# Modulation weights of a two-block transformer: as halves in activation tiles, one column group ahead, instead of through the ring of raw weight tiles

## Chip, cores and metric

One Trainium2 chip, one core. The metric is the device time of the slowest core (here the only one), in microseconds (us); the median of several runs is given. The granted clock of TensorE is told as a share of full speed, 2.4 GHz; its other level is 1.2 GHz.

## What is computed

`reference` chains two blocks over 256 tokens of width 1024, in float32. The first block (two layers: FFN, RWKV and block-sparse attention mixer, cross attention, FFN) is the same before and after. The second block is the one with modulation:

```python
mod_lat = (silu(c) @ w_mod[i] + b_mod[i])[:, None, :]
mod_ctx = (silu(c_ctx) @ w_mod[i] + b_mod[i])[None, None, :]
sh1, sc1, gt1, sh2, sc2, gt2 = split(mod_lat, 6, axis=-1)
csh1, csc1, cgt1, csh2, csc2, cgt2 = split(mod_ctx, 6, axis=-1)
...
x_lat = x_lat + gt1 * mix
x_lat = x_lat + gt2 * sq_relu_mlp(modulate(rms_norm_2(x_lat, g_norm2[i]), sh2, sc2), w_mlp1[i], w_mlp2[i])
```

It has two layers (i = 0, 1), 256 latent tokens and 256 context tokens. `w_mod` is 2 x 1024 x 6144 float32, 50 MB of weights that are multiplied by two vectors only. `mix` is a grouped-query attention, a low-rank attention and a pooling, concatenated and projected by `w_out`. The context is not updated in the last layer.

## The kernel before

The kernel is bound by matmuls in float32 accuracy: each product is three passes, `mm3` (L537, L538, L539), on operands split into a high and a low part. Weights stream from HBM in tiles of 128 x 1024 (512 KB). `raw` (L484) takes a tile from a ring of four (NRAW) and issues its DMA on SP's queue (L486); `wsplit` makes the high part on ScalarE (L513) and the low part on VectorE (L514), three pairs at a time; then the matmuls use them. SP issues in order: a load that waits for its tile holds up the loads behind it.

The modulation weights are read by `mod_vectors(l, half)` (L1388). A half of a layer has 12 column groups, so there are 48 groups in all, numbered here 0 to 47 over (0,0), (0,1), (1,0), (1,1). Before, a group is two raw tiles, from the same ring of four, and they are not split: eight float32 matmuls (L1399) read them directly, with the two small vectors as the 32-column operand, four of them side by side in four column quadrants of PE (`tile_position`):

```python
ws = [self.raw(self.t["mod"][(l * 24 + n) * 2 + kc]) for kc in range(2)]
for kc in range(2):
    for q in range(4):
        nc.tensor.matmul(ps[32 * q:32 * q + 32, :S], self.cs[:, 4 * kc + q, ...],
                         ws[kc][:, q * S:q * S + S], ..., tile_position=(0, 32 * q))
```

A matmul in float32 leaves two records in the trace, so a whole group is one row with x16. After the twelfth group of a half the sums are copied, transposed and added to the bias.

Where the groups stand: the generator is a background stream. `wload` (L489 to L499) advances it by a count of units at each weight tile (`due`), so one group comes with every few weight tiles. The halves (0,0), (0,1) and what fits of (1,0) run so in the first block's FFNs and mixers (`early`, L1362); the rest of (1,0) in the first MLP of the second block (L1997). The last half, (1,1), is a side stream (`modulation`, L2032 to L2036) of the weave of the second block's second layer (L2038), which interleaves projections, attention, keys, queries and pooling. Its result is needed after the last out projection, `mix_out(1, lat)` (L2040), by the norm ahead of the last MLP (`lat["h"].finish()`, L2041).

The order on each engine is not the program's: a scheduler places instructions by priority and by when it expects operands and pool slots to be free. A tile that is to be written waits until the slot's earlier reader is done. The activation pool (`b2`, L415) has 55 slots (NB2) of 128 x 512 (256 KB); hidden activations, keys, queries and probabilities live there.

Of the kernel before, what the change touches and what calls it, by code (L numbers as in the profile page):

```python
# [19 lines left out]
S = 256  # L20
# [1350 lines left out]
class Second(First):  # L1371
# [16 lines left out]
    def mod_vectors(self, l, half, bank=None):  # L1388

        nc = self.nc  # L1390
        bank = bank or self.at_ps
        for n in range(12 * half, 12 * half + 12):
            m = n % MG
            if m == 0:
                ps = bank()
            ws = [self.raw(self.t["mod"][(l * 24 + n) * 2 + kc]) for kc in range(2)]
            for kc in range(2):
                for q in range(4):
                    nc.tensor.matmul(ps[32 * q:32 * q + 32, :S], self.cs[:, 4 * kc + q, 32 - 2 * m:64 - 2 * m],  # L1399
                                     ws[kc][:, q * S:q * S + S], start=m == 0 and kc == 0,  # L1400
                                     stop=m == MG - 1 and kc == 1, tile_position=(0, 32 * q))
            if m < MG - 1:
                yield 2 * self.mpace
                continue
            sb = self.t1()
            nc.scalar.activation(sb, ps[:, :S], AF.Copy)
            yield U
            pt = bank()
            for b in range(2):
                nc.tensor.matmul(pt[:, 32 * b:32 * b + 32], sb[:, b * P:(b + 1) * P], self.cst("sel32"),  # L1410
                                 start=True, stop=True)
            for b in range(2):
                blocks = slice(2 * (n - m) + b, 2 * n + b + 1, 2)
                nc.vector.tensor_tensor(self.mods[l][:, blocks],
                                        pt[:, 32 * b:32 * b + 2 * MG].rearrange("p (m i) -> p m i", i=2),
                                        self.vec(f"b_mod{l}")[:, blocks].unsqueeze(2).to_broadcast([P, MG, 2]),
                                        op=ALU.add)
            yield 2 * self.mpace - U
            if n - m <= 12 * half + 7 <= n:
                o, i = 24 * half + 8, half + 1  # L1420
                self.gm[l][i] = g = self.cp.tile([P, KD, 2], F32, name=f"gm{i}_{l}")
                nc.vector.scalar_tensor_tensor(g, self.mods[l][:, o:o + 8], 1.0,
                                               self.vec(f"g_norm{i}{l}").unsqueeze(2).to_broadcast([P, KD, 2]),
                                               op0=ALU.add, op1=ALU.mult)
        self.modulated.add((l, half))
# [650 lines left out]
```

## Time and profile before

| | us |
|---|---|
| median of 3 runs | 2471.49 (2471.09 to 2473.09) |
| the profiled execution | 2474.53 |
| its span in the profile | 2472.7 |
| mean granted clock in it | 0.983 |

The profile shows one execution, and its rows are in us from the start of the span. In it a busy time is that of the instructions of one engine; an idle time stands in brackets behind the instruction that came after it, with what released it ("<-DMA raw<-in_mod_dram": the load of a modulation tile). Rows of matmuls overlap, so the start of the next row tells more than a row's duration. A window row gives a stretch and its length, then the busy time and the instructions (x) of PE, PEld, DVE, ACT and POOL in it, then PE's granted clock, the busy share of the DMA engines and their GB/s. PEld is the load of PE's stationary operand.

### The profile page before, as it was taken

Reading aid. Unit: us, or ns where it says so; the run is one execution under the profiler, and the core shown is the slowest. Engines: PE = TensorE matmul, PEld = TensorE weight load, DVE = VectorE, ACT = ScalarE, POOL = GpSimd, SP = SyncE. Lnnn points to the kernel's source line nnn. Section 1 sums busy time; section 2 is a strip of 40 time slices with the busy share of each in tenths; the row PEclk is TensorE's granted clock in tenths of the full one; section 3 lists DMA queues with packets and bytes.
Section 4 is the critical chain, followed back from the end, with each engine's and each line's share of the span. In section 5 each row is a group of like instructions: output and inputs, shape, how many; then the busy total and the mean of one; then the engine's idle time right before and its main releaser. Section 6 shows DMA issues by size and latency. Waiting matters only on the chain. (4 is left out here: it accounts for less than half of the span.)

```text
span 2472.7 us, 52358 instructions
## 1 busy us (share of the span) xinstructions
PE 2373.1 (96%) x21745; PEld 2254.9 (91%) x21745; DVE 1627.8 (66%) x2883; ACT 1187.2 (48%) x2025; POOL 260.4 (11%) x396
## 2 busy tenths in 40 slices
PE   8999999999999999999999999879999999788999
PEld 7998889999999998889999989869999999668999
DVE  6756767666556657757686777877753447776665
ACT  5544346544444445355554565556542235454443
POOL 2210101011001101001021121120100003021000
PEclk9999999999999999999999999989999999889999
DMA  6766333467776775334455534412672226442554
GB/s 217 225 224 201 118 107 101 142 189 229 223 237 220 224 231 170 100 99 121 137 182 168 176 120 137 142 60 86 195 231 95 93 87 214 154 131 69 179 179 146
DMA packets 115310, 393.17 MB, mean 159 GB/s; under 512 B 12864, under 2 KB 16704, under 8 KB 115072
## 3 DMA queue, kind: packets, MB, share of 16 engines
q1 hardware_dynamic: 113920, 388.15, 49.5%
q8 instruction: 171, 2.80, 0.4%
q10 hardware_dynamic: 1152, 1.67, 0.2%
q14 instruction: 67, 0.55, 0.1%
HBM read 388.71 MB, written 3.16 MB: 158 GB/s over the span
## 5 line engine op out<-in xcount | busy, mean ns | idle before, releaser
L537 PE MATMUL mm<-b,wh 128*128 128x256 f32 x4792 | 1375.6, 288 | 21.4 <-ACT wh L518 7.7
L538 PE MATMUL mm<-b,wh 128*128 128x256 f32 x4792 | 1364.1, 285 | 1.4 <-DVE b L531 1.4
L539 PE MATMUL mm<-b,wl 128*128 128x256 f32 x4792 | 1361.5, 284 | 3.0 <-DVE wl L514 2.8
L513 ACT ACTIVATE wh<-raw 128x1024 fp32r<-128x1024 f32 (+2 forms) x637 | 658.1, 1034 | 889.7 <-PE mm L538 470.3
L514 DVE TENSOR_TENSOR wl<-raw,wh 128x1024 fp32r<-128x1024 f32 (+2 forms) x637 | 766.6, 1205 | 448.0 <-ACT wh L513 442.5
L537 PEld LDWEIGHTS mm<-b,wh 128*128 128x128 f32 x4792 | 921.9, 193 | 48.4 <-issue 18.9
L539 PEld LDWEIGHTS mm<-b,wl 128*128 128x128 f32 x4792 | 922.6, 193 | 6.2 <-DVE wl L514 4.5
L538 PEld LDWEIGHTS mm<-b,wh 128*128 128x128 f32 x4792 | 923.1, 193 | 4.1 <-DVE b L531 2.6
L639 POOL TENSOR_TENSOR t<-t,t 128x256 f32<-128x256 f32 x85 | 85.4, 1007 | 896.3 <-ACT t L636 895.6
L518 ACT ACTIVATE b<-t 128x256 fp32r<-128x256 f32 (+1 forms) x192 | 86.4, 462 | 111.4 <-POOL t L789 66.2
L519 DVE TENSOR_TENSOR b<-t,b 128x256 fp32r<-128x256 f32 (+1 forms) x192 | 93.8, 498 | 57.4 <-ACT b L518 57.3
L789 POOL TENSOR_TENSOR t<-t,t 128x256 f32<-128x256 f32 x88 | 71.3, 810 | 468.5 <-DVE t L787 422.8
L784 DVE TENSOR_TENSOR t<-mm,rb 128x512 f32<-128x512 f32 x88 | 60.6, 689 | 35.3 <-PE mm L539 33.9
L537 PE MATMUL mm<-wh,b 128*128 128x256 f32 (+2 forms) x272 | 81.5, 302 | 1.6 <-ACT wh L513 1.1
L538 PE MATMUL mm<-wl,b 128*128 128x256 f32 (+2 forms) x272 | 80.0, 295 | 0.8 <-DVE wl L514 0.8
L539 PE MATMUL mm<-wh,b 128*128 128x256 f32 (+2 forms) x272 | 79.1, 294 | 0.5 <-DVE b L376 0.5
L537 PE MATMUL at<-b,b 64*128 64x256 f32 (+3 forms) x216 | 66.7, 315 | 9.9 <-ACT b L654 4.9
L538 PE MATMUL at<-b,b 128*128 128x256 f32 (+3 forms) x240 | 69.2, 293 | 0.0
L1399 PE MATMUL at<-raw,cs 128*32 128x256 f32 x768 | 60.5, 396 | 8.5 <-DMA raw<-in_mod_dram 8.5
L654 ACT ACTIVATE b<-at,mx 128x512 f32<-128x512 f32 (+1 forms) x88 | 51.2, 587 | 32.2 <-DVE mx L1303 17.9
L1839 DVE SCALAR_TENSOR_TENSOR x<-mm,mods,x 128x256 f32<-128x256 f32 x80 | 38.5, 482 | 41.6 <-PE mm L539 41.4
L539 PE MATMUL at<-b,b 64*128 64x256 f32 (+3 forms) x216 | 62.2, 294 | 1.1 <-DVE b L519 1.1
(296 smaller groups left out, 2518.0 us busy)
## 6 DMA issues: line engine op xcount, KB each, us to landing
raw<-in_ffn_in_dram SPq DMA_DIRECT2D x175, 512.0 KB, 4.0
raw<-in_mlp_dram SPq DMA_DIRECT2D x160, 512.0 KB, 3.4
raw<-in_mod_dram SPq DMA_DIRECT2D x96, 512.0 KB, 4.1
raw<-in_ffn_out_dram SPq DMA_DIRECT2D x64, 512.0 KB, 4.3
raw<-in_mix_in_dram SPq DMA_DIRECT2D x52, 512.0 KB, 3.9
raw<-in_xkv_dram SPq DMA_DIRECT2D x32, 512.0 KB, 3.6
raw<-in_ffn_out_dram SPq DMA_DIRECT2D x32, 384.0 KB, 3.4
raw<-in_out_dram SPq DMA_DIRECT2D x24, 512.0 KB, 4.0
```

The lines of the kernel that those rows point to most:

```text
L513: nc.scalar.activation(wh[:, :width], raw[:, :width], AF.Copy)
L514: nc.vector.tensor_tensor(wl[:, :width], raw[:, :width], wh[:, :width].bitcast(F32), op=ALU.subtract)
L518: self.nc.scalar.activation(h, src, AF.Copy)
L519: self.nc.vector.tensor_tensor(l, src, h.bitcast(F32), op=ALU.subtract)
L537: mm(out, a[0], b[0], start=first, stop=False)
L538: mm(out, a[0], b[1], start=False, stop=False)
L539: mm(out, a[1], b[0], start=False, stop=last)
L639: eng.tensor_tensor(sqs[0], sqs[0], sq, op=ALU.add)
L654: nc.scalar.activation(p, s, AF.Exp, scale=scale, bias=neg, accum_out=sm)
L784: nc.vector.tensor_tensor(gu, self.pair(ps), self.over2(norm.rb), op=ALU.mult)
L789: nc.gpsimd.tensor_tensor(hv, th, gu[:, 1], op=ALU.mult)
L1399: nc.tensor.matmul(ps[32 * q:32 * q + 32, :S], self.cs[:, 4 * kc + q, 32 - 2 * m:64 - 2 * m], ws[kc][:, q * S:q * S + S], start=m == 0 and ...
```

## The change

A group is now four tiles of the activation pool (`b2`, 128 x 2 x 256, 256 KB each, half a raw tile), each with a DMA of its own (L1397 of the changed kernel). `load(n + 1)` is called ahead of the matmuls of group n; the first group of each half is loaded in the step that uses it. The eight matmuls of a group (L1408 now) are the same, with the same values. The ring of raw tiles holds only split weights. Lines behind this place are 9 higher.

```diff
@@ -1389,15 +1389,24 @@
 
         nc = self.nc
         bank = bank or self.at_ps
+
+        def load(n):
+            ws = [self.b2() for _ in range(4)]
+            for i, w in enumerate(ws):
+                src = self.t["mod"][(l * 24 + n) * 2 + i // 2][:, i % 2 * 512:i % 2 * 512 + 512]
+                nc.sync.dma_start(w, src.rearrange("p (a s) -> p a s", a=2))
+            return ws
+
+        nxt = load(12 * half)
         for n in range(12 * half, 12 * half + 12):
             m = n % MG
             if m == 0:
                 ps = bank()
-            ws = [self.raw(self.t["mod"][(l * 24 + n) * 2 + kc]) for kc in range(2)]
+            ws, nxt = nxt, load(n + 1) if n < 12 * half + 11 else None
             for kc in range(2):
                 for q in range(4):
                     nc.tensor.matmul(ps[32 * q:32 * q + 32, :S], self.cs[:, 4 * kc + q, 32 - 2 * m:64 - 2 * m],
-                                     ws[kc][:, q * S:q * S + S], start=m == 0 and kc == 0,
+                                     ws[2 * kc + q // 2][:, q % 2], start=m == 0 and kc == 0,
                                      stop=m == MG - 1 and kc == 1, tile_position=(0, 32 * q))
             if m < MG - 1:
                 yield 2 * self.mpace
```

The three places below show what becomes of it on PE and on SP. On the whole of PE, the modulation matmuls stood in 58 runs without another matmul between them, 37 of them of eight; now they stand in 84, 33 of eight and 36 of two. On ScalarE, VectorE and GpSimd the order hardly moves but in the weave of the second layer, where the splits of the first three out weights move ahead.

First place: PE, `ffn2` of layer 0 (around 637 us), the opening group of half (0,1), group 12. `mm` is a projection's accumulator, `b` its activations, `wh` and `wl` the split weight, `at` the modulation sums, `cs` the two vectors. Before:

```order
L538 MATMUL mm_8182<-b_1136_7015,wh_8185 128x256
L539 MATMUL mm_8182<-b_1136_7015,wl_8186 128x256
L1399 MATMUL at_8262<-raw_8263,cs 32x256 x4
L1399 MATMUL at_8262<-raw_8265,cs 32x256 x4
L537 MATMUL mm_8253<-b_1094_6750,wh_8215 128x256
L538 MATMUL mm_8253<-b_1094_6750,wh_8215 128x256
```

Now:

```order
L539 MATMUL mm_8399<-b_1118_6823,wl_8362 128x256
L1408 MATMUL at_8318<-b_1363_8310,cs 32x256 x2
L537 MATMUL mm_8399<-b_1124_6861,wh_8361 128x256
L538 MATMUL mm_8399<-b_1124_6861,wh_8361 128x256
L539 MATMUL mm_8399<-b_1124_6861,wl_8362 128x256
L1408 MATMUL at_8318<-b_1364_8311,cs 32x256 x2
L537 MATMUL mm_8399<-b_1130_6899,wh_8361 128x256
```

A pair of matmuls per tile, three or six projection matmuls between the pairs, where one run of eight stood. Groups 0 (some 135 us) and 24 (some 852 us) move in the same way.

Second place: PE at the end of the last half. Before, groups 45 (its end), 46 and 47 in attention (some 2185 to 2190 us; `at` on L1399 is the modulation sum, the other `at` are scores):

```order
L538 MATMUL at_27372<-b_4385_26566,b_4518_27169 128x256
L539 MATMUL at_27372<-b_4385_26566,b_4519_27170 128x256
L1399 MATMUL at_25956<-raw_28162,cs 32x256 x2
L1399 MATMUL at_25956<-raw_28172,cs 32x256 x4
L1399 MATMUL at_25956<-raw_28174,cs 32x256 x4
L1399 MATMUL at_25956<-raw_28184,cs 32x256 x4
L1399 MATMUL at_25956<-raw_28186,cs 32x256 x4
L537 MATMUL at_27400<-b_4469_26935,b_4518_27169 128x256
L538 MATMUL at_27400<-b_4469_26935,b_4518_27169 128x256
```

Now group 43 and those behind it, in `mix_out(1, lat)` (from some 2249.5 us on), between the products of the first out weight:

```order
L537 MATMUL mm_28409<-b_4842_28166,wh_28399 128x256
L1408 MATMUL at_26108<-b_4872_28300,cs 32x256 x2
L538 MATMUL mm_28409<-b_4842_28166,wh_28399 128x256
L539 MATMUL mm_28409<-b_4842_28166,wl_28400 128x256
L537 MATMUL mm_28409<-b_4857_28233,wh_28399 128x256
L1408 MATMUL at_26108<-b_4873_28301,cs 32x256 x2
L538 MATMUL mm_28409<-b_4857_28233,wh_28399 128x256
L539 MATMUL mm_28409<-b_4857_28233,wl_28400 128x256
L537 MATMUL mm_28409<-b_4662_27534,wh_28399 128x256
L538 MATMUL mm_28409<-b_4662_27534,wh_28399 128x256
L539 MATMUL mm_28409<-b_4662_27534,wl_28400 128x256
```

Groups 43 to 47, 20 pairs, go on like this through the first five of the projection's eight weights. Before, no modulation matmul stands in that projection. Groups 39, 41 and 42 move a little inside attention (42 in runs of two and six); groups 7 and 31 are cut into runs in the first block, 31 some 400 to 780 us earlier than it stood.

Third place: SP, the loads around the end of the weave. Before, the last nine of 14 modulation tiles (groups 41 to 47, behind the last u tile), then the first of the 8 out weights:

```order
L486 DMA raw_28138<-in_mod_dram 128x1024
L486 DMA raw_28148<-in_mod_dram 128x1024
L486 DMA raw_28150<-in_mod_dram 128x1024
L486 DMA raw_28160<-in_mod_dram 128x1024
L486 DMA raw_28162<-in_mod_dram 128x1024
L486 DMA raw_28172<-in_mod_dram 128x1024
L486 DMA raw_28174<-in_mod_dram 128x1024
L486 DMA raw_28184<-in_mod_dram 128x1024
L486 DMA raw_28186<-in_mod_dram 128x1024
L486 DMA raw_28205<-in_out_dram 128x1024
L486 DMA raw_28211<-in_out_dram 128x1024
L486 DMA raw_28245<-in_out_dram 128x1024
```

Now:

```order
L486 DMA raw_27405<-in_u_dram 128x576
L486 DMA raw_27466<-in_u_dram 128x576
L486 DMA raw_28397<-in_out_dram 128x1024
L486 DMA raw_28403<-in_out_dram 128x1024
L486 DMA raw_28437<-in_out_dram 128x1024
L486 DMA raw_28472<-in_out_dram 128x1024
L486 DMA raw_28507<-in_out_dram 128x1024
L1397 DMA b_4596_27310<-in_mod_dram 128x512
L1397 DMA b_4597_27311<-in_mod_dram 128x512
L1397 DMA b_4598_27312<-in_mod_dram 128x512
L1397 DMA b_4599_27313<-in_mod_dram 128x512
L486 DMA raw_28542<-in_out_dram 128x1024
```

Behind the four tiles of group 41 come two more out weights, then the 24 tiles of groups 42 to 47, each of which waits for a slot of the activation pool, then the eighth out weight and the MLP's weights. The out weights passed ten modulation tiles and more; the modulation tiles fell behind them.

## Rows read from the trace of the kernel before

**Rows 1.** The page's part 1: busy us (share of the span) x instructions.

```profile
PE 2373.1 (96%) x21745; PEld 2254.9 (91%) x21745; DVE 1627.8 (66%) x2883; ACT 1187.2 (48%) x2025; POOL 260.4 (11%) x396
```

**Rows 2.** Windows: an FFN stretch, the weave's end in four, the out projection.

```profile
530.00:930.00 400.00, 399.29 (x3457) 382.56 (x3456) 240.29 (x327) 176.38 (x255) 40.40 (x56) 1.00 0.71 226
2120.00:2166.00 46.00, 38.60 (x278) 31.49 (x279) 32.98 (x96) 19.86 (x36) 4.12 (x6) 0.88 0.60 191
2166.00:2185.00 19.00, 19.00 (x126) 11.94 (x125) 10.39 (x21) 10.78 (x24) 2.72 (x4) 0.93 0.53 160
2185.00:2193.00 8.00, 2.92 (x39) 1.06 (x37) 7.21 (x28) 2.10 (x5) 2.70 (x6) 0.97 0.81 297
2193.00:2247.00 54.00, 50.31 (x352) 46.08 (x352) 42.32 (x93) 39.41 (x88) 6.87 (x8) 0.91 0.12 39
2247.00:2271.00 24.00, 23.86 (x197) 23.67 (x198) 13.07 (x17) 9.93 (x15) 7.09 (x5) 1.00 0.42 132
```

**Rows 3.** PE's waits, whole run: us, times, the longest.

```profile
PE at L1399 <- DMA raw<-in_mod_dram: 8.5, 7, 2.5
```

**Rows 4.** PE's timeline in the weave: start us, us, instruction, idle before and releaser.

```profile
2120.45 0.72 PE L1399 MATMUL at<-raw,cs 128*32 128x256 f32 x8 [0.62 <-DMA raw<-in_mod_dram]
...
2123.08 1.06 PE L1399 MATMUL at<-raw,cs 128*32 128x256 f32 x2 [1.91 <-DMA raw<-in_mod_dram]
...
2161.99 1.08 PE L1399 MATMUL at<-raw,cs 128*32 128x256 f32 x8 [2.52 <-DMA raw<-in_mod_dram]
...
2165.20 1.30 PE L1508 MATMUL wk<-ct,b 128*128 128x128 f32 x5 [0.82 <-DVE b L1478]
...
2189.66 0.64 PE L1399 MATMUL at<-raw,cs 128*32 128x256 f32 x8 [2.38 <-DMA raw<-in_mod_dram]
...
2193.04 0.58 PE L537 MATMUL at<-b,b 64*128 64x256 f32 x1 [2.75 <-ACT b L654]
```

**Rows 5.** PE's timeline in an FFN: a whole group between two projection matmuls.

```profile
146.23 0.28 PE L539 MATMUL mm<-b,wl 128*128 128x256 f32 x1
146.44 1.07 PE L1399 MATMUL at<-raw,cs 128*32 128x256 f32 x16
147.44 0.39 PE L537 MATMUL mm<-b,wh 128*128 128x256 f32 x1
147.67 0.28 PE L538 MATMUL mm<-b,wh 128*128 128x256 f32 x1
```

**Rows 6.** PE's timeline in attention: a run of four matmuls, then a single one.

```profile
2181.10 0.29 PE L539 MATMUL at<-wh,b 128*128 128x288 f32 x1
2181.32 0.64 PE L1399 MATMUL at<-raw,cs 128*32 128x256 f32 x8
...
2182.13 0.29 PE L538 MATMUL at<-wl,b 128*128 128x288 f32 x1
...
2183.57 0.28 PE L539 MATMUL at<-b,b 64*128 64x256 f32 x1
2183.78 0.62 PE L1399 MATMUL at<-raw,cs 128*32 128x256 f32 x2
...
2184.55 0.28 PE L538 MATMUL at<-b,b 64*128 64x256 f32 x1
```

**Rows 7.** DMA issues (KB, median us to landing); then the context's 256 KB loads.

```profile
raw<-in_mod_dram SPq DMA_DIRECT2D x96, 512.0 KB, 4.1
...
DMA to landing us min/median/max: 4.4/6.2/6.4
```

**Rows 8.** Window, the modulation matmuls (L1399) alone: PE, PEld, clock, DMA share, GB/s.

```profile
2166.00:2185.00 19.00, 6.68 (x44) 1.63 (x44) 0.93 0.53 160
```

**Rows 9.** SP's timeline: start us, us, load, instructions.

```profile
2152.77 33.45 SPq L486 DMA_DIRECT2D raw<-in_mod_dram  x14
```

**Rows 10.** ScalarE's timeline at the first out weight.

```profile
2190.90 1.06 ACT L513 ACTIVATE wh<-raw 128x1024 fp32r<-128x1024 f32 x1 [6.94 <-DMA raw<-in_out_dram]
```

**Rows 11.** The page's part 5, the low part of a weight: busy, mean ns, idle before.

```profile
L514 DVE TENSOR_TENSOR wl<-raw,wh 128x1024 fp32r<-128x1024 f32 (+2 forms) x637 | 766.6, 1205 | 448.0 <-ACT wh L513 442.5
```

## The prediction, made before the changed kernel ran

> **What bounds the kernel now.** I read the page's first part first: TensorE (PE) is busy 96% of the span [rows 1]. So time can only come from PE's gaps, from work taken off PE, or from a granted clock below 1.00. The windows say where each is the case. In an FFN stretch PE is busy 399.29 of 400 us at a granted clock of 1.00 [rows 2]: there the kernel is bound by matmuls alone, whatever the loads do. The same holds for the last out projection, 2247 to 2271: 23.86 of 24 us. Only the second layer's weave in between is loose: from 2120 to 2247 PE is busy 38.60 of 46, 19.00 of 19, 2.92 of 8 and 50.31 of 54 us, at granted clocks of 0.88, 0.93, 0.97 and 0.91 [rows 2]. The reader should see two kinds of place: stretches where a load can gain nothing and a costlier matmul costs its full price, and one weave where waits can be won.
>
> Then the waits of PE: the modulation matmuls wait for their loads 8.5 us in all, in 7 places, 2.5 at most [rows 3]. That is 0.3% of the time, and it is all that loading earlier can give directly; the four longest, 7.4 of the 8.5 us, lie in the weave [rows 4].
>
> **Price of a modulation run on PE.** A group is eight matmuls (16 records), and the chip runs the four column quadrants side by side. In an FFN the matmul ahead of a whole group starts at 146.23 and the second after it at 147.67, 1.44 us [rows 5]. Ordinary matmuls follow each other by 0.12 us (399.29 us by 3457, [rows 2]), so two steps are 0.24 and the group adds 1.20 us. A run of four matmuls (x8 records): 2181.10 to 2182.13, 1.03 us; a run of one (x2 records): 2183.57 to 2184.55, 0.98 us [rows 6]. Less the two steps, each adds 0.74 to 0.79. So a short run costs about 0.74 however little is in it: two more quadrants beside the first are free, and most of the price is that of going over to the 32-column form and back. The Trainium skill, TensorEngine Tiling (Array Packing), section Key Properties, says that a change of tiling mode drains the TensorE; the rows of the short runs agree, and the rule speaks against this change, which goes over 26 times more. By the rule the sum below stands; without it (a pair at its share) it would be that of rival S.
>
> A pair of matmuls (what a 256 KB tile feeds) lies between the run of one and the run of four: I take 0.74. A group split in four pairs among other matmuls costs 4 x 0.74 = 2.96 instead of 1.20: +1.76.
>
> **The change, part by part.**
>
> 1. *Opening groups 0, 12 and 24.* Each half's first load is issued in the step that uses it, and the order then places the four pairs apart, between the projection's matmuls (first place of the order above). All three lie in FFNs, where PE has no gap [rows 2]: 3 x 1.76 = **+5.3**.
> 2. *Their landing.* Four 256 KB loads issued together landed after 4.4 to 6.4 us where the context does this [rows 7]; a 512 KB modulation load after 4.1 (median). PE's place for the pairs was chosen by a schedule, so it may wait. Bounds 0 (landed in time) and 6.9 (three halves, each the 2.3 between 4.1 and 6.4): **+1.0**, near the lower end, since no modulation load in an FFN is waited for now.
> 3. *Groups 43 to 47.* Before, they stand in the weave; now their 20 pairs stand in the out projection (second place), one between nearly every other product. That stretch is PE-bound at full clock, so each pair costs its whole price: 20 x 0.74 = **+14.8**. Nothing covers it: the next stage, the MLP, needs the projection's last column.
> 4. *Their loads.* They stand behind the seven first out weights on SP and wait for slots of the activation pool, which attention still holds (third place). PE may reach the first pair before it has landed. Bounds 0 and 6.4 [rows 7]: I take **+2.5**, below the middle, as only the first of a row of loads is late by its whole latency. A further +0.5 (0 to 1.1) is for the copy of the sums behind the last group, by half of a row of ScalarE [rows 10].
> 5. *Groups 7 and 31* are cut into two more runs in PE-bound stretches: up to 3 x 0.74 less shared columns, **+1.8** (bounds 0 and 2.2). Group 42 goes into attention in two runs: **+1.0** (0 to 1.5).
> 6. *Weave, waits that go.* At group 39 the 0.62 and 1.91 us [rows 4] go, now that these loads are not behind the ring: **-2.5** (0 to -2.5). The 2.52 us ahead of group 42 go too, but right behind them PE waits 0.82 us for DVE's L1478 [rows 4], so DVE's chain is late next: 0.
> 7. *Weave, work that leaves.* From 2166 to 2185 PE is busy all the time, 6.68 us of it with modulation [rows 8]. If that leaves, DVE (10.39 of 19) and ACT follow soon: **-2** (0 to -6.7).
> 8. *Weave, out weights earlier.* Before, SP issues 14 modulation loads from 2152.77, 33.45 us long, and the out weights only behind them [rows 9]. So ACT stands 6.94 us at the first out weight's split until 2190.90, with attention's copies behind it [rows 10], and PE waits 2.38 for a load and 2.75 for ACT [rows 4]. Now five out weights come ahead. But DVE is busy 7.21 of these 8 us [rows 2], so little of it can be saved: **-2.5** (0 to -5.1). The splits that now come earlier put DVE work ahead of attention's, one low part by 1.205 us [rows 11]: **+1.2** (0 to 3.6, for three).
> 9. *Granted clock.* From 2120 to 2247 it is below 1.00: 46 x 0.12 + 19 x 0.07 + 8 x 0.03 + 54 x 0.09 = 12 us of full-speed PE time is lost [rows 2]. It is low just where PE has gaps, and if the waits of 6 and 8 go, part of it returns; gaps that only move take the low clock along. **-3** (+3 to -12).
>
> All other groups keep their places on PE; their loads, one group ahead, leave SP a little earlier, and PE waited for none of them but those in the weave: 0. Were that cover gone (a pool slot late), a wait of the size in [rows 3], up to 2.5 us, could appear in each half.
>
> Sum: 5.3 + 1.0 + 14.8 + 2.5 + 0.5 + 1.8 + 1.0 - 2.5 - 2 - 2.5 + 1.2 - 3 = **+18.1**. The profiled execution took 2474.53, so 2492.6; the median of the runs is 3.0 lower, 2471.49, so I give **2489**. No change, as far as a measurement tells, is within 0.2%, 5 us: 2466.5 to 2476.4.
>
> **The rivals.**
>
> *F, faster: the ring was the weave's bound.* With the modulation loads out of the ring, everything in the weave moves up: 8.5 us of load waits, 2.75 for ACT, 6.7 of modulation out of 2166 to 2185 and the 12 us of clock, together -30, against the 20.1 of points 1 and 3, which the order fixes: 2474.5 - 10 - 3 = **2462**. For it: ACT's 6.94 us and the SP burst. Against it: in 2185 to 2193 DVE is busy 90%, and behind the 2.52 us wait DVE is the next releaser. It decides from 25 us of gain in the weave on.
>
> *S, no change: a pair costs only its share.* If the change of form is paid by the weights loaded and not by the run, a pair is a quarter of 1.20, 0.30. Then point 1 is 0 and point 3 is 6.0, points 5 some 1.5; with the others as above +2.7, **2474**. For it: a group's matmuls in parallel quadrants cost little. Against it: the run of one at 0.74.
>
> *L, slower still: the out projection starves.* The 20 loads that wait for attention's slots are 5.2 MB. Before's burst moved 14 x 0.52 MB in 33.45 us, 219 GB/s: 24 us, about what the projection with its pairs takes. If they move at the 132 GB/s of that stretch [rows 2], it is 40 us, some 12 to 14 more: **2501**. The last out weight and the MLP's first stand behind them on SP.
>
> *The change doesn't do what it says*: opening groups have no lead, and from 42 on the lead is the pool's to give. That is in the forecast, not beside it.
>
> **How the numbers follow.** Forecast (a short run costs its full 0.74, weave gains under 15 us): 0.59. L 0.18. S 0.12. F 0.11. Faster is F alone: 0.11. Within 0.2% is S: 0.12. Slower: 0.77. The range leaves out F and the tail of L: 2469 (S, with the weave's gains some 5 larger) to 2502. The forecast's own range is 2479 to 2497.
>
> **What would show it.** Right: in the out projection (some 40 us long instead of 24) runs of x4 records, each with 0.98 us from the matmul ahead to the second one behind; the three opening groups in FFNs likewise; no wait left at group 39; ACT's 6.94 us gone; weave shorter by 5 to 15 us. Wrong: pairs that add 0.3 us (S); a weave shorter by 25 us and more (F); long waits for modulation loads in the out projection, or for MLP weights behind it (L).

## The result, and the profile after

| | before | after |
|---|---|---|
| median of the runs, us | 2474.99 (6 runs) | 2498.47 (2494.86 to 2502.19, 6 runs) |
| profiled execution, us | 2474.53 | 2497.81 |
| its span, us | 2472.7 | 2496.0 |

The change makes the kernel slower: a ratio of 1.0091, 95% interval 1.0077 to 1.0106, some 23 us. The forecast was 2489, its stated range 2469 to 2502, the forecast's own range 2479 to 2497.

Part 1 of the page after, as [rows 1]. PE has 20 us more to do, with the same instructions:

```profile
PE 2393.1 (96%) x21745; PEld 2262.3 (91%) x21745; DVE 1629.4 (65%) x2883; ACT 1187.9 (48%) x2025; POOL 253.7 (10%) x396
```

PE's waits after, whole run (us, times, longest), as [rows 3]. The waits for modulation loads fell from 8.5 to 1.7 us, as the change would have it. But a wait for VectorE's L1487 has come up, 6.9 us in one piece, where before no wait for L1478, the same instruction, was longer than 2 us:

```profile
PE wk L1517 <- DVE b L1487: 10.6, 4, 6.9
...
PE at L1408 <- DMA b<-in_mod_dram: 1.7, 3, 0.7
```

To see where the time came in I took the starts of the same matmuls in both traces and their difference, after less before. It grows by 2.8, 2.3 and 2.5 us in the three FFN stretches with an opening group (**7.6**; the first is counted from the start of the span to 229 us). All other places up to the second layer's weave (some 2090 us) take back **4.4**; from there to the first matmul of the out projection it grows by **5.3**; in that projection by **15.3**; behind it nothing (-0.4). Together 23.3, but for rounding.

The out projection after, from PE's timeline: ordinary steps of 0.12 us, then pairs, each with 0.99 us from the start of the matmul ahead to the start of the second one behind (2257.89 to 2258.88):

```profile
2257.78 0.28 PE L539 MATMUL mm<-b,wl 128*128 128x256 f32 x1
2257.89 0.28 PE L537 MATMUL mm<-b,wh 128*128 128x256 f32 x1
2258.10 0.63 PE L1408 MATMUL at<-b,cs 128*32 128x256 f32 x4
2258.66 0.38 PE L538 MATMUL mm<-b,wh 128*128 128x256 f32 x1
2258.88 0.28 PE L539 MATMUL mm<-b,wl 128*128 128x256 f32 x1
2259.00 0.28 PE L537 MATMUL mm<-b,wh 128*128 128x256 f32 x1
2259.21 0.63 PE L1408 MATMUL at<-b,cs 128*32 128x256 f32 x4
```

The modulation loads for it, SP's timeline after: all are issued by 2246.8, 9 us before the projection begins (2255.6), and no pair waits. What rival L feared did not come:

```profile
2204.50 42.33 SPq L1397 DMA_DIRECT2D b<-in_mod_dram  x24
```

Three windows of after (PE, PEld, DVE, ACT, POOL, PEclk, DMA share, GB/s): the middle of the weave, from the start of the last projection weight's last matmul there to the first scores that use the next split weight; from there to the out projection; the out projection.

```profile
2156.40:2180.70 24.30, 14.36 (x67) 7.62 (x65) 17.79 (x46) 7.33 (x14) 6.82 (x9) 0.58 0.28 95
2180.70:2255.60 74.90, 62.66 (x423) 54.40 (x423) 53.25 (x127) 46.89 (x105) 7.17 (x13) 0.86 0.29 99
2255.60:2294.90 39.30, 39.27 (x284) 28.12 (x283) 13.44 (x19) 10.31 (x16) 5.02 (x5) 1.00 0.25 81
```

The same three, between the same matmuls, in the kernel before:

```profile
2155.00:2174.30 19.30, 14.59 (x110) 6.48 (x108) 15.08 (x42) 4.48 (x10) 6.84 (x9) 0.82 0.74 256
2174.30:2247.10 72.80, 63.93 (x464) 55.00 (x463) 55.28 (x133) 49.09 (x109) 9.58 (x13) 0.93 0.25 81
2247.10:2271.10 24.00, 23.96 (x197) 23.77 (x198) 12.97 (x16) 9.93 (x15) 7.09 (x5) 1.00 0.42 132
```

So the projection went from 24.0 to 39.3 us, busy all the time at full clock, and the middle of the weave from 19.3 to 24.3, with 21 of its 37 modulation matmuls gone and a granted clock of 0.58 in place of 0.82. The part behind it went from 72.8 to 74.9, at 0.86 in place of 0.93. PE's timeline there, after:

```profile
2160.36 0.88 PE L1517 MATMUL wk<-ct,b 128*96 128x128 f32 x3 [0.56 <-DVE b L1507]
2168.10 0.87 PE L1517 MATMUL wk<-ct,b 128*128 128x128 f32 x3 [6.86 <-DVE b L1487]
...
2176.26 0.41 PE L537 MATMUL at<-b,b 64*128 64x256 f32 x1
2176.47 0.41 PE L538 MATMUL at<-b,b 64*128 64x256 f32 x1
...
2200.01 0.47 PE L1814 MATMUL wk<-ct,b 128*128 128x128 f32 x1 [7.38 <-DVE b L531]
```

Before, in the same gap ahead of L1508, PE had four runs of modulation matmuls from 2157.24 on, each after a wait for its load (2.52 us the longest), and last waited 0.82 us for L1478 [rows 4]. Now it waits 6.86, and behind that its matmuls follow each other by 0.21 us, half the speed. The same happens once more. Before, from 2185.2 us on, 18 modulation matmuls and waits of 2.38 and 2.75 us [rows 4] stood ahead of the next scores; now PE waits 7.38 us for VectorE there, and from the last matmul ahead of the gap to those scores it is 8.2 us where it was 8.0. VectorE's chain in the first gap is as long as before but starts later, by 1.5 us against the matmul at which the window starts: one low part of an out weight now stands ahead of it (as in the 1.23 us of the L514 row; three of these splits moved forward):

```profile
2157.77 1.23 DVE L514 TENSOR_TENSOR wl<-raw,wh 128x1024 fp32r<-128x1024 f32 x1 [0.19 <-ACT wh L513]
2158.92 1.83 DVE L1507 SCALAR_TENSOR_TENSOR b<-b,rc 128x192 f32<-128x192 f32 x8
```

### The profile page after: what moved, and what is told of

Read it like the earlier page. It is cut to its first block, busy times and chain, and to the rows that moved or that the text cites. A ratio compares the mean times of both kernels' runs of the same rounds, so it can differ in the third digit from the quotient of the medians.

```text
span 2496.0 us, 52473 instructions
## 1 busy us (share of the span) xinstructions
PE 2393.1 (96%) x21745; PEld 2262.3 (91%) x21745; DVE 1629.4 (65%) x2883; ACT 1187.9 (48%) x2025; POOL 253.7 (10%) x396
## 5 line engine op out<-in xcount | busy, mean ns | idle before, releaser
L514 DVE TENSOR_TENSOR wl<-raw,wh 128x1024 fp32r<-128x1024 f32 (+2 forms) x637 | 767.2, 1206 | 444.0 <-ACT wh L513 438.3
L1408 PE MATMUL at<-b,cs 128*32 128x256 f32 x768 | 71.1, 392 | 1.7 <-DMA b<-in_mod_dram 1.7
```

Source lines behind the costliest of these rows:

```text
L514: nc.vector.tensor_tensor(wl[:, :width], raw[:, :width], wh[:, :width].bitcast(F32), op=ALU.subtract)
```

## The experiments

**Whole groups instead of pairs (e1).** The one thing changed is the order of a group's four loads:

```diff
-            for i, w in enumerate(ws):
+            for i, w in reversed(list(enumerate(ws))):
```

> The changed kernel with the four loads of a group issued in the opposite order, the last half first. A group's first matmul then waits for the load that lands last, so the order on PE keeps groups whole: 59 runs of modulation matmuls in place of 84, at nearly the same places, with the same tiles, slots and loads. Theory (a short run costs its full price): the openings lose 3 x (4 x 0.65 - 1.09) = 4.5 us, the out projection 20 x 0.77 less 5 x 1.20 = 9.4 us; 12 to 14 us less than the changed kernel, a ratio to the kernel before near 1.004, and the out projection about 31 us long in place of 40. Rival L (the out projection starves for its loads): the time stays within 3 us of the changed kernel, and the waits for the loads grow by what the runs save. Rival S: within 3 us too, without such waits.

Measured: 2490.03 us, ratio 1.0059 (1.0044 to 1.0074), against 1.0091 for the change. The windows of the weave's middle and of the out projection, and a row of an opening group with its wait:

```profile
2159.80:2181.70 21.90, 11.37 (x61) 6.95 (x59) 17.03 (x46) 7.34 (x14) 6.84 (x9) 0.61 0.30 101
2256.80:2287.10 30.30, 30.30 (x285) 26.52 (x283) 13.39 (x19) 10.34 (x17) 5.04 (x5) 1.00 0.32 105
```

```profile
138.83 1.07 PE L1408 MATMUL at<-b,cs 128*32 128x256 f32 x16 [1.39 <-DMA b<-in_mod_dram]
```

The projection's 39.3 became 30.3 us: 9.0 less, against 9.4 expected, at the same place, with the same bytes and slots, and without a wait. Rivals L and S fall there: what the pairs cost is the number of runs. The openings give 3.4 (7.6 to 4.2) and not 4.5, as a whole group waits for its last load (1.39, 1.10 and 1.23 us). The total falls by 8 and not by 12 to 14. In the profile the middle of the weave gives another 2.4 us (21.9 in place of 24.3, with one modulation run in place of three behind the gap), but two places take back more. Around group 39, at 2090 to 2130 us, 3.4 are lost. A stretch at some 1650 us took 31 us in place of 26, at a granted clock of 0.77 in place of 0.92 (a net 3.2, as 1.6 are won just ahead of it). It holds no changed instruction; it is long in e3, e4 and e5 too, and short in the kernel before, the change, e2, e6, e7 and e8. Whether the kernel or the execution decides it is not shown. So I compare windows, not totals, where a few us matter.

**The last half back in the ring (e2).** Groups 36 to 47 are loaded as before; the others as in the change:

```diff
+            if (l, half) == (1, 1):
+                rs = [self.raw(self.t["mod"][(l * 24 + n) * 2 + kc]) for kc in range(2)]
+                ws = [rs[i // 2][:, i % 2 * 512:i % 2 * 512 + 512].rearrange("p (a s) -> p a s", a=2) for i in range(4)]
```

> The changed kernel with the last half (groups 36 to 47) loaded through the ring of raw tiles again. Theory: what is lost from 2100 us on is lost by these groups alone, so only the openings and the small shifts of the first three halves are left, 3 us by the comparison of the two traces at 2100 us: a ratio to the kernel before of 1.001 (2 to 5 us more). Rival: the weave itself is slower by the way its tiles are shared now, then more than 8 us stay.

Measured: 2481.32, ratio 1.003 (1.002 to 1.0041): 5 to 10 us more than the kernel before by the runs, above the 2 to 5 expected; 2.6 by the profile's span, 2475.3. The profiled execution is the shortest of its ten, 4.3 us under their median, and what those 4.3 are is not shown. The rival's 8 and more in the weave are ruled out by the three windows:

```profile
2157.00:2176.30 19.30, 14.39 (x109) 6.39 (x107) 14.81 (x42) 4.52 (x10) 6.84 (x9) 0.82 0.75 253
2176.30:2249.10 72.80, 64.61 (x465) 55.26 (x464) 56.10 (x133) 49.10 (x109) 9.12 (x13) 0.91 0.24 81
2249.10:2273.10 24.00, 24.00 (x199) 23.82 (x199) 12.93 (x16) 9.93 (x15) 7.09 (x5) 1.00 0.42 131
```

All three are as long as in the kernel before, to 0.1 us: the loss from the middle of the weave on belongs to these twelve groups, and the openings' part to the others (8.4 us of it still there, by the starts).

**A ring of their own (e3).** Tiles of 512 KB, two of them, one group ahead; the activation pool has 51 slots.

```diff
-NB2 = 55
+NB2 = 51
...
-            ws = [self.b2() for _ in range(4)]
+            ws = [self.wp.tile([P, WC], F32, tag="mod", name=self.nm("mod"), bufs=2) for _ in range(2)]
```

> Modulation tiles of 512 KB in a ring of their own of two, one group ahead, with the activation pool cut from 55 to 51 slots to make room. Whole groups, no pairs, no place in the out projection. Theory: 17 to 25 us less than the changed kernel, and against the kernel before -3 to +3 us, as the weave is bound by VectorE's chain and not by the ring. Rival F (the common ring was the weave's bound): 10 us or more faster than the kernel before.

Measured: 2480.72, ratio 1.0024 (1.0014 to 1.0033): 18 us below the change, as expected, but 6 above the kernel before, not -3 to +3. In its profile (span 2479.2, 6.5 above) 5.2 us are the stretch at 1650 us of e1, another 5.2 are lost in the weave, and other places give 3.9 back. The middle of the weave, and PE's waits for the ring:

```profile
2156.60:2180.40 23.80, 16.10 (x84) 7.64 (x82) 17.09 (x46) 7.34 (x14) 6.83 (x9) 0.60 0.48 159
```

```profile
PE at L1407 <- DMA mod<-in_mod_dram: 11.9, 9, 3.4
```

With the common ring free of modulation the weave is not faster, and the middle of it is nearly as slow as in the change (23.8), with PE's gaps and a clock of 0.60 again. Alone this doesn't rule out rival F, since PE still waits 11.9 us for the small ring and the activation pool has lost four slots. But the change, in which no modulation matmul of the weave waits for its load, is 5.3 us slower there: with both, F falls.

**Filling the gap (e4, e5).** Behind group 40 stand matmuls that nothing needs; they add work, and no result depends on them:

```diff
+            if (l, half, m) == (1, 1, 4):
+                fp = self.mm_ps()
+                for i in range(NFILL):
+                    nc.tensor.matmul(fp[:, :S], self.x[i % 4][:, :P], self.x[4 + i % 4], start=True, stop=True)
```

> The changed kernel with 14 float32 matmuls of 128x256 behind group 40, on residual tiles and into a PSUM tile that nothing reads; they add work and change nothing in the result. They lie where PE waits 6.86 us for VectorE's L1487, after which the granted clock is 0.57 for 15 us. Theory: the modulation runs that stood there before were cover that kept the clock up; with the filler the clock of that stretch goes to 0.9 and more, and the time falls by 3 to 6 us against the changed kernel. Rival: VectorE and ScalarE bind that stretch at either clock; then nothing is gained, or the filler costs up to 2 us.

Measured with 14: 2500.93, ratio 1.01 (1.0083 to 1.0118), no gain. It did not do what it was for: the filler ended early and PE still waited 3.71 us, so the clock fell all the same (0.74 over the window, 23.2 us long, and 0.50 from 2172 to 2180). That left the question open, so the next has 23.

> As e4_filler, with 23 of these matmuls instead of 14. In e4_filler 14 took 6.3 us from 2160.9 on, and PE then still waited 3.71 us for L1487's counterpart; the granted clock behind it was 0.50 for 8 us, so that the run did not do what it was for. 23 should take 10.4 us and reach to within 1 us of the end of VectorE's chain. Theory (the clock behind the gap is a cost of its own): granted clock 0.9 and more from 2171 to 2185, and the stretch up to the first scores of the next projection is 2 to 4 us shorter than in the changed kernel, the four short transposes that now come later taking back 1 us. Rival: the stretch is bound by VectorE and ScalarE at either clock; it is no shorter, and the filler costs 1 us.

Measured: 2494.62, ratio 1.0079 (1.0062 to 1.0096), beside the change itself, run once more (e7).

> The changed kernel once more, on the chip and in the call of the runs beside it, so that e5_filler_long is compared with it directly: a ratio to the kernel before of 1.008 to 1.0105. No theory is tested.

e7 gave 2499.84, ratio 1.01 (1.0086 to 1.0115). The middle of the weave in e5, then in e7:

```profile
2161.60:2181.00 19.40, 18.08 (x115) 13.72 (x114) 16.52 (x45) 5.58 (x11) 6.83 (x9) 1.00 0.37 122
```

```profile
2157.40:2181.80 24.40, 14.46 (x70) 7.95 (x68) 17.92 (x48) 7.35 (x14) 6.82 (x9) 0.59 0.28 98
```

```profile
2163.11 10.20 PE L1415 MATMUL mm<-x 128*128 128x256 f32 x46
...
2175.20 0.98 PE L1522 MATMUL wk<-ct,b 128*128 128x128 f32 x7 [1.32 <-DVE b L1492]
```

With 10 us of useless work the stretch is 5.0 us shorter, 19.4 as in the kernel before, at a granted clock of 1.00 instead of 0.59; more than the 2 to 4 expected. The medians differ by 5 us too, though the intervals overlap; the two profiled executions differ by 2.4 only, as e5's is the one with the long stretch at 1650 us. VectorE's chain did not become shorter: PE's wait for it still ends the gap. What became shorter is what lies behind the gap. The end of that chain, in the kernel before, the change and e5:

```profile
2165.88 0.91 DVE L1478 TENSOR_TENSOR b<-b,b 128x384 f32<-128x384 f32 x1
2168.77 0.89 DVE L1487 TENSOR_TENSOR b<-b,b 128x384 f32<-128x384 f32 x1
2174.25 0.90 DVE L1492 TENSOR_TENSOR b<-b,b 128x384 f32<-128x384 f32 x1
```

From there to the first scores (2174.28, 2180.74, 2181.17) it is 7.5, 11.1 and 6.0 us, with 13, 8 and 8 modulation matmuls. So of the 5.0 us that the change lost here 1.5 are VectorE's later start and the rest the low clock, which also hid what the five matmuls less would have won. The modulation matmuls that the change took out of the gap had been cover: they cost nothing there and helped to keep the clock up.

**The kernel before, its two tiles in the opposite order (e6).** The order trick of e1 applied to the ring:

```diff
-            ws = [self.raw(self.t["mod"][(l * 24 + n) * 2 + kc]) for kc in range(2)]
+            ws = [self.raw(self.t["mod"][(l * 24 + n) * 2 + kc]) for kc in (1, 0)][::-1]
```

> The kernel before with the two raw tiles of a group loaded and used in the opposite order, second half of the rows first; ring, sizes and places as before. On PE the groups of the weave lie in fewer runs (53 in place of 58, group 43 in runs of 1, 6 and 1 instead of 1, 3, 1, 3, groups 45 to 47 with 19 in one run). Theory: five short runs less, 5 x 0.74 = 3.7 us at most, all in a weave that VectorE bounds: 0 to 3 us faster than the kernel before, within 0.2%. Rival F (the weave is bound by PE's modulation work): 4 us or more.

Measured: 2478.8, ratio 1.0013 (1.0002 to 1.0024): no gain. By the profile it loses 3.6 us in the second part of the weave (76.4 in place of 72.8, at a granted clock of 0.87 in place of 0.93). In the middle it is as long as before, 19.3, though only two runs in place of five stand behind VectorE's chain:

```profile
2156.10:2175.40 19.30, 13.98 (x94) 7.84 (x86) 15.14 (x42) 5.33 (x11) 6.84 (x9) 0.65 0.56 195
```

The granted clock there is 0.65 in place of 0.82, so I read it that the low clock took back what the fewer runs saved. Both theories missed; why the second part loses was not followed up.

**The kernel before, with its last norm filled (e8).** The low clock behind a gap, tried at another place:

```diff
         lat["h"].finish()
+        fp = self.mm_ps()
+        for i in range(12):
+            nc.tensor.matmul(fp[:, :S], self.x[7][:, :P], self.x[6], start=True, stop=True)
```

> The kernel before, with 12 float32 matmuls of 128x256 on residual tiles, into a PSUM tile that nothing reads, in the waits of PE in the last norm (2 ahead of its sums' last products, 6 behind them, 2 and 2 further on); the result stays as it is. In the kernel before PE waits 1.05, 2.42, 0.52 and 1.20 us there, and the granted clock is 0.50 to 0.53 from 2277 to 2285 us. Theory (a gap's low clock is a cost of its own, and work without use can buy it off): the granted clock there goes to 0.9 and more, and the stretch from the projection's end to the fourth MLP weight is 1.5 to 3 us shorter; the whole time 0.1% lower, at the edge of what can be measured. Rival: the low clock comes with this place, whatever PE does; the stretch is the same or longer by up to 1 us.

From the projection's last matmul into the first MLP weights, first the kernel before, then e8:

```profile
2271.10:2288.10 17.00, 11.83 (x70) 10.82 (x69) 10.56 (x31) 5.80 (x11) 0.00 (x0) 0.70 0.19 62
```

```profile
2269.30:2284.20 14.90, 14.20 (x95) 12.65 (x94) 10.57 (x31) 5.85 (x11) 0.00 (x0) 1.00 0.23 71
```

2.1 us shorter, as expected. The whole, 2475.26 at a ratio of 1.0 (0.9989 to 1.0012), can't be told from the kernel before. No version here beats it measurably.

## Why the prediction was right, point by point

**Points 1 and 2, the openings: 6.3 forecast, 7.6 measured.** The pairs cost what they were priced at, and the three waits for the first load 0.66, 0.40 and 0.68 us, 1.7 in place of 1.0. The last of the four loads lands 1.1 to 1.4 us too late for a whole group (e1). The landing varies: in e7, the same kernel, the second group's first load is waited for 1.66 us, the granted clock from 630 to 650 us falls to 0.91, and that stretch grows by 5.0 us in place of 2.3.

**Point 3, the pairs in the out projection: 14.8 forecast, 15.3 measured.** A pair is 0.99 less 0.24, 0.75 us, and 20 of them 15.0. e1 shows the mechanism: five runs of eight there cost 6.3. What the 0.75 is made of the prediction had wrong: it put most of it to the change of form. But a run of eight costs 1.20 and a run of four 0.79 [rows 5, rows 6], so four more matmuls in the same quadrants cost 0.41, and e5's float32 matmuls, which change no form, take 0.44 each (10.2 us for 23). By these rows some 0.4 of a run of one to four is the matmuls' own time, side by side in their quadrants, and some 0.3 is left for the change of form; that is an estimate. A group in four pairs pays the 0.4 four times instead of twice, and the 0.3 four times instead of once. The Trainium skill (TensorEngine Tiling (Array Packing), Key Properties) says that a change of tiling mode drains the TensorE; a remainder of some 0.3 us per run agrees with it, and it gives no price.

**Point 4, late loads: 3.0 forecast, none measured.** I took it that attention would hold the slots to its end. The tiles came free earlier: the loads ran from 2204.5 to 2246.8.

**Point 5: 2.8 forecast; the remainder of the first 2090 us is -4.4.** Two parts of it can be named: 361.5 to 367.8 before, at a granted clock of 1.00, takes 9.1 us after at 0.62, +2.8; 1118 to 1143 before, at 0.93, takes 22.2 after at 1.00, -2.8. They cancel, and neither holds a modulation matmul. That such differences come without any change is seen in e8, in whose profile the first of these two stretches is long as well, and there the kernel is still the one before. Group 31, which left the second block's MLP, and what follows it give -1.6. The split of the rest was not followed.

**Points 6 to 9, the weave: -8.8 forecast, +5.3 measured. This is the step that failed.** The 5.3 are -1.8 around group 39, +5.0 in the middle and +2.1 behind it. Point 6 came in part: no wait at group 39. It also saw that behind the 2.52 us VectorE's chain is next, and put that at 0. But the 0.82 us wait of [rows 4] says that the gap up to 2165.20 is VectorE's, so that the runs in it were cover; without them it is one gap of 6.86 us, and a second one of 7.38 follows. Point 7 took the modulation out of 2166 to 2185, behind the gap, as a gain of 2. At full clock there is one (6.0 us in e5 where the kernel before has 7.5), but the change had the low clock there and took 11.1. Point 8's cost of one low part came, 1.4 us on VectorE's chain; ScalarE's first out splits came earlier, and PE's wait for VectorE stayed. Point 9 had the wrong sign. It expected the clock to recover when load waits go; instead short waits became long ones, and the 12 us behind the first ran at the low clock. Filling that gap gives 5.0 us back (e5).

The errors partly cancel (weave 14 too low, late loads and point 5 some 10 too high), so the total, 18.1 against 23.3 in the profiles, is nearer than its parts. That is luck, and so in part is the range: 2498.47 lies above the forecast's own 2479 to 2497, and inside the stated one only because that reached up towards rival L, which did not come. 3.5 of the 9.5 us by which it exceeds 2489 are the kernel before, 2474.99 by six runs where three had given 2471.49. Of the rivals, S fell by the rows of the pairs and by e1, L by SP's row, F by e3 and the weave itself.

## What to carry to other kernels

Interleaving a few matmuls of another array form into a stream that is bound by PE costs per run and not per matmul: here 0.75 us for one, two or four of them, which run side by side, and 1.20 for eight. If a group's operands come in several loads, let its first matmul need the load that lands last; one word in the load loop was worth 9 us in the projection. And before work is taken from a stretch where PE looks busy, look for what ends PE's next wait: work that fills a wait for another engine was free here, and its loss can cost the clock behind the gap as well.

## What the runs showed of the hardware that I had not expected

Useless work made a stretch faster: with 23 matmuls in a gap of 6.9 us the stretch around it took 5.0 us less (24.4 to 19.4), with 12 in the last norm 2.1 less (17.0 to 14.9); the granted clock went from 0.59 and 0.70 to 1.00. Behind a gap of 3.71 us that was left (e4) it was 0.50 again. And the low clock comes to the same instructions in some executions and not in others. Here is one stretch of 112 matmuls, in the kernel before and in e8, which up to there is the same kernel:

```profile
361.50:367.80 6.30, 5.86 (x112) 5.16 (x112) 5.89 (x24) 6.10 (x19) 0.00 (x0) 1.00 0.49 161
361.60:370.40 8.80, 8.38 (x112) 7.46 (x112) 6.76 (x26) 6.51 (x19) 0.00 (x0) 0.63 0.35 114
```

2.5 us, a tenth of the whole effect studied here. Over the whole span the granted clock of the kernel before is 1.7% below full (0.983). The Trainium skill (TensorE: Matmul & The Clock Gate, Part 1: The HAM clock gate) puts the penalty of the clock's ramp below 1% of a typical kernel's span. For the ramp at the start this trace agrees: in the kernel before, PE's matmuls follow each other by 0.21 us from 7.66 to 10.5 us and by 0.12 from 11.9 on, so less than 2 us are lost, 0.1%.
